# One more of the 22 gated pairs of the second feed-forward in seven products, its input sums beside one plain pair

## Chip, core and metric

The program runs on one core of a Trainium2 chip. The metric is the device time of one execution in microseconds (us), from the first instruction to the last and what lies around them. Lower is better. All inputs and outputs are fp32 and lie in the chip's memory.

The engines are named as the profile names them: PE multiplies matrices, DVE and ACT work on vectors (ACT also evaluates functions), POOL and SP here mostly start transfers. Every engine works through its own list of instructions in order.

## The reference

One step of a two-layer encoder over 1088 positions (1024 of a prompt, 64 of a sample) with 1024 channels. Layer 0 mixes by attention, layer 1 by a state-space model and a gated linear unit (GLU). Each layer then has a gated feed-forward with a causal convolution of width 3. The change is in the feed-forward of layer 1 and in what is prepared for it:

```python
def conv_ffn(h, prev, w_up, conv_w, conv_b, w_down):
    t = h.shape[1]
    up = h @ w_up
    full = jnp.concatenate([prev.astype(up.dtype), up], axis=1)
    c = conv_b
    for j in range(CONV_WIDTH):
        c = c + conv_w[j] * full[:, j:j + t]
    y = (jax.nn.gelu(c[..., :D_FF]) * c[..., D_FF:]) @ w_down
    return y, full[:, -(CONV_WIDTH - 1):]
...
    hp = rms_norm(xp, g_pre_ffn[i])
    fp, cpi = conv_ffn(hp, zeros, w_up[i], conv_w[i], conv_b[i], w_down[i])
    xp = xp + rms_norm(fp, g_post_ffn[i])
```

`w_up` is 1024 x 5632: 2816 gate columns and 2816 value columns, which are 22 + 22 tiles of 128. A gate tile f and its value tile 22 + f are a **pair**.

## The kernel before

Channels lie on the 128 partitions and positions along the free axis, in three blocks of 384, 384 and 320 positions. An fp32 factor is split into a high and a low half (`hh` and `hl` for the activations, the two halves of `whl` for a weight tile), and `mm3` (L221 to L225) makes a product of three matmuls: high weights by low activations (L223), high by high (L224), low weights by high activations (L225). The low half of a weight tile is made by DVE (L216) after ACT has made the high half, so the first two matmuls of a product can start without DVE and the third cannot. Weights come through `unit` (L166), which keeps two units loaded ahead through two buffers `raw` and six buffers `whl`.

**Plain pair** (`up`, `up_block`, L404 to L433): for each tile and block, 8 x 3 matmuls into one of six PSUM buffers `mm`; DVE then multiplies by the norm's factor `rb` (L414, L416) and thereby frees the buffer. `conv` (L418 to L425) follows with one pass on ACT and two on DVE (L423, L424), `gate` (L435) multiplies the two tiles (L440) and POOL stores the result to `gd`.

**Pair in seven products** (`seven`, L496): for the first two blocks (768 positions as two halves of 384, 1024 channels as two halves of 512) the 2 x 2 x 2 block product is made of seven products in place of eight, by sums of the inputs and sums of the weights. The third block stays plain. Sums of the inputs are made once, on DVE: `normed` (L462) multiplies the activations by the norm, `input_sums` (L470) makes four differences (L478) and the split of one of them, `into_place` (L483) splits the other operands into high and low (`split`, L458: ACT makes the high half at L459, DVE the low half at L460). Four of these overwrite `hh` and `hl` of the first two blocks, from which the plain pairs read until then. Sums of the weights are made during the GLU before it, by jobs of two halves per pair (`sums`, L1388): POOL loads `sj` (L1392), DVE makes four sums (L1396 to L1399), POOL stores them to `su` (L1400). One job starts with each of the 48 steps of the GLU (`beside`, L1405), and its sums stand two steps later; the GLU uses 34 such steps for 17 pairs.

The constant `PLAIN` (L29) says how many pairs are plain. In the loop over f in `ffn` (L537) with `PLAIN` = 5: pair 1 is plain; before pair 2 the first two blocks are normed; before pair 3 `input_sums` is issued; pair 4 is issued as two interleaved tiles (`up([f, KF + f])`, L543), then `into_place` and the norm of the third block; from pair 5 on every pair is `seven`, and the first of these still uses the third block as it was and is followed by the split of its normed form.

The order on each engine is made by the framework's scheduler from priorities and a timeline that it simulates while the program is built; the code fixes single edges (`order`, L112).

Of the kernel before, what the change touches and what calls it, by code (L numbers as in the profile page):

```python
# [25 lines left out]
LOW = 1500  # L26
SIDE = 32

PLAIN = 5  # L29

KCUT = (0, 12, 22)
GT = [[(4, "blkA")] * 3, [(4, "blkB"), (4, "blkB"), (2, "big")]]
# [11 lines left out]
class Core:  # L44
    def __init__(self, ctx, tc, a):
# [5 lines left out]
        for i in range(2):  # L51
            for m in range(KF):
                sums = [("w_sum", m, e) for e in range(2)] if i == 1 and m >= PLAIN else []
                self.wsrc += [("w_up", i, m)] + sums + [("w_up", i, m + KF)]
# [285 lines left out]
    def ffn(self, i, h, rb, after, side=None, beside=lambda: None, x=None, g=None):  # L340
# [12 lines left out]
        def sums_w(k):  # L353
            x = (jt[:, :2048] if i == 0 else self.yp.tile([P, 2048], F32, name="jw", tag="ypB", bufs=1)).rearrange("p (c h m) -> p c h m", c=2, h=2)
            Q.dma_start(x, a["w_down"][i, k::KH].rearrange("c p (h m) -> p c h m", h=2))
            yield
            a11, a12, a21, a22 = x[:, 0, 0], x[:, 1, 0], x[:, 0, 1], x[:, 1, 1]
            E.tensor_add(a22, a21, a22)
            E.tensor_sub(a21, a11, a21)
            E.tensor_sub(a11, a22, a11)  # L360
            E.tensor_sub(a12, a12, a11)
            Q.dma_start(sd[:, k], x)
# [16 lines left out]

        w0 = (PLAIN + 1) * i  # L380
        starts = {2 * (k + w0) + 1: sums_w(k) for k in range(KH)}
# [45 lines left out]
        def up(ms):  # L427

            wu = {m: up_start(m) for m in ms}
            for b in range(3):  # L430
                for w, u in wu.values():
                    up_block(w, u, b)
            return {m: u for m, (w, u) in wu.items()}  # L433
# [28 lines left out]
        def normed(bs):  # L462

            for b in bs:
                t0, n = BLK[b]
                for k in range(KD):
                    v = nc.vector.scalar_tensor_tensor(x[b][:, k], x[b][:, k], g[:, k:k + 1], rb[:, t0:t0 + n], op0=ALU.mult, op1=ALU.mult)
                    self.order(v, self.last_conv)

        def input_sums():  # L470

            V = nc.vector
            b11, b21, b12, b22 = (half(x[b], j) for b in range(2) for j in range(2))
            t1, t4 = (self.big([P, 4, 384], "t", F32) for _ in range(2))
            t2 = ts.tile([P, 4, 384], F32, name="t2", tag="t2")
            for o, u, v in ((t1, b12, b11), (b12, b22, b12), (t2, b22, t1), (t4, b21, t2)):
                for k in (slice(0, 2), slice(2, 4)):
                    self.order(V.tensor_sub(o[:, k], u[:, k], v[:, k]), self.last_conv)  # L478
            op["t1"] = [ts.tile([P, 4, 384], F32R, name=f"t1{j}") for j in range(2)]
            split(*op["t1"], t1)  # L480
            return t2, t4
# [14 lines left out]
        def seven(f, first):  # L496
            V = nc.vector
            ug, uv = u_tile(f), u_tile(KF + f)
            g0, g1, v0, v1 = (u[:, 2 + 384 * j:386 + 384 * j] for u in (ug, uv) for j in range(2))

            def product(w, j, o, sums=False):
                ps = self.mm_ps()[:, :384]
                for k in range(4):
                    c = (k // 2 * 4 + 2 * j + k % 2 if sums else 4 * j + k) * P
                    self.mm3(ps, w, slice(c, c + P), op[o][0][:, k], op[o][1][:, k], k == 0, k == 3)
                return ps
            w = self.unit(("w_up", i, f))
            if first:
                up_block(w, ug, 2)
            nc.scalar.activation(g1, product(w, 0, "b11"), AF.Copy)  # L510
            V.tensor_add(g0, g1, product(w, 1, "b21"))
            ws = self.unit(("w_sum", f, 0))
            V.tensor_add(g1, g1, product(ws, 0, "t2", True))
            p3 = product(ws, 1, "b22", True)
            if not first:
                up_block(w, ug, 2, True)
            ws = self.unit(("w_sum", f, 1))
            V.tensor_add(v1, g1, product(ws, 0, "t3", True))
            V.tensor_add(g1, g1, p3)
            p5 = product(ws, 1, "t1", True)  # L520
            V.tensor_add(g1, g1, p5)  # L521
            w = self.unit(("w_up", i, KF + f))
            V.tensor_add(v0, v1, product(w, 1, "t4"))
            V.tensor_add(v1, v1, p5)
            up_block(w, uv, 2, not first)
            return {f: ug, KF + f: uv}
# [10 lines left out]
        for f in range(1, KF):  # L537
            if i == 1 and f == 2:
                normed((0, 1))
            if i == 1 and f == 3:  # L540
                late = input_sums()
            if i == 1 and f == PLAIN - 1:
                us = up([f, KF + f])  # L543
                into_place(*late)
                normed((2,))
            if i == 1 and f >= PLAIN:
                us = seven(f, f == PLAIN)
                if f == PLAIN:
                    for j in range(2):
# [1060 lines left out]
```

## Time and profile before

| | us |
|---|---|
| median of 3 runs (2247.86 to 2254.37) | 2248.89 |
| the profiled execution | 2243.39 |
| its span, first to last instruction | 2241.6 |
| PE busy in the span | 2188.9 (98%) |
| DVE busy in the span | 1687.4 (75%) |
| ACT busy in the span | 1019.1 (45%) |

Times in the trace are counted from the first instruction. The GLU runs from about 1300 to 1492, the second feed-forward's plain pairs from 1492 to 1616, its pairs in seven products from 1616 to about 1988, and its down-projection after that. A row of the timeline has the start, the length, the engine, line and operation, what it writes and reads, and in brackets how long the engine was idle before it and what released it. Matmuls overlap one another by half their length, so the pace of PE is read from the distance of their starts, not from the length of one. On DVE, too, the next instruction starts up to 0.1 us before the end of the one ahead of it.

### The profile page before, as it was taken

How to read it: one execution, taken by the hardware profiler on the slowest of the kernel's cores; microseconds unless marked ns; L12 is line 12 of the kernel's file. 1: busy time of each engine (PE TensorE's matmuls, PEld its weight loads, DVE VectorE, ACT ScalarE, POOL GpSimd, SP SyncE). 2: the span in 40 equal slices, each digit the busy share in tenths (PEclk: the TensorE clock that was granted, in tenths of full speed). 3: DMA queues.
4: the chain of work that ended last, by engine and by line, in shares of the span. 5: the costliest groups of instructions: out<-in, count | busy, mean ns of one | idle time of the engine just before them, and what ended most of it. 6: DMA issues, size and time to landing. Idle time of an engine off the chain costs nothing.

```text
span 2241.6 us, 36077 instructions
## 1 busy us (share of the span) xinstructions
PE 2188.9 (98%) x13875; PEld 2114.0 (94%) x13875; DVE 1687.4 (75%) x2954; ACT 1019.1 (45%) x1839; POOL 414.7 (18%) x474
## 2 busy tenths in 40 slices
PE   9999999999999999999998899999999999999997
PEld 8987789999999999999996699999999999999997
DVE  8687648989877877666768865587997788786754
ACT  5256747422333333455534742263444444455543
POOL 5322004200042323100200034352011111110000
PEclk9999999999999999999999999999999999999999
DMA  5100015656345565887749998751266667678773
GB/s 197 38 22 29 20 62 158 246 184 211 111 136 183 181 192 184 253 298 232 229 147 340 272 295 297 261 167 65 96 217 223 236 237 276 209 269 310 224 243 99
DMA packets 208124, 428.48 MB, mean 191 GB/s; under 512 B 23312, under 2 KB 114224, under 8 KB 205008
## 3 DMA queue, kind: packets, MB, share of 16 engines
q1 hardware_dynamic: 175648, 326.56, 44.3%
q0 software_dynamic: 23984, 95.12, 11.9%
q10 hardware_dynamic: 8320, 4.49, 0.9%
q8 instruction: 109, 1.79, 0.3%
q14 instruction: 63, 0.52, 0.1%
HBM read 297.75 MB, written 128.37 MB: 190 GB/s over the span
## 4 chain that ended last, share of the span: by engine, by line
PE 47%; DMA 6%; DVE 5%; ACT 1%; issue 1%; SPq 1%; POOL 0%; DVEq 0%; ACTq 0%; POOLq 0%
PE mm L225 12%; PE mm L223 12%; PE mm L224 12%; DMA raw<-in_w_down 3%; PE pb L223 1%; PE pb L225 1%; PE pa L224 1%; PE pb L224 1%; PE pa L225 1%; PE pa L223 1%; DVE whl L216 1%; ACT whl L216 1%; DMA yd<-ys 1%; DMA pm<-prm 1%; DVE y L328 0%
## 5 line engine op out<-in xcount | busy, mean ns | idle before, releaser
L223 PE MATMUL mm<-hl,whl 128*128 128x384 f32 (+1 forms) x1960 | 643.4, 329 | 3.8 <-DVE hl L306 3.1
L225 PE MATMUL mm<-hh,whl 128*128 128x384 f32 (+1 forms) x1960 | 641.1, 328 | 2.2 <-DVE whl L216 2.2
L224 PE MATMUL mm<-hh,whl 128*128 128x384 f32 (+1 forms) x1960 | 642.3, 328 | 0.0
L223 PEld LDWEIGHTS mm<-hl,whl 128*128 128x128 f32 x1960 | 368.5, 188 | 6.0 <-DVE hl L306 4.5
L225 PEld LDWEIGHTS mm<-hh,whl 128*128 128x128 f32 x1960 | 368.5, 188 | 2.9 <-DVE whl L216 2.9
L224 PEld LDWEIGHTS mm<-hh,whl 128*128 128x128 f32 x1960 | 368.7, 188 | 0.0
L216 ACT ACTIVATE whl<-raw 128x1024 fp32r<-128x1024 f32 x202 | 212.9, 1058 | 333.4 <-PE mm L225 192.2
L216 DVE TENSOR_TENSOR whl<-raw,whl 128x1024 fp32r<-128x1024 f32 x202 | 254.9, 1264 | 111.2 <-ACT whl L216 110.7
L223 PE MATMUL mm<-gt,whl 128*128 128x384 f32 (+1 forms) x968 | 316.8, 327 | 2.6 <-ACT whl L216 1.7
L225 PE MATMUL mm<-gt,whl 128*128 128x384 f32 (+1 forms) x968 | 315.8, 327 | 0.7 <-DVE whl L216 0.7
L224 PE MATMUL mm<-gt,whl 128*128 128x384 f32 (+1 forms) x968 | 315.9, 327 | 0.0
L223 PEld LDWEIGHTS mm<-gt,whl 128*128 128x128 f32 x968 | 181.7, 188 | 3.2 <-ACT whl L216 1.9
L225 PEld LDWEIGHTS mm<-gt,whl 128*128 128x128 f32 x968 | 181.6, 188 | 1.2 <-DVE whl L216 1.2
L224 PEld LDWEIGHTS mm<-gt,whl 128*128 128x128 f32 x968 | 181.7, 188 | 0.0
L194 DVE TENSOR_TENSOR whl<-raw,whl 128x1024 fp32r<-128x1024 f32 x84 | 96.3, 1153 | 69.2 <-ACT whl L193 68.2
L193 ACT ACTIVATE whl<-raw 128x1024 fp32r<-128x1024 f32 x84 | 82.6, 987 | 115.0 <-DMA raw<-sd 50.2
L423 DVE SCALAR_TENSOR_TENSOR t<-u,ppt,t 128x1090 f32<-128x1090 f32 x88 | 123.6, 1407 | 7.9 <-ACT t L422 7.3
L422 ACT ACTIVATE t<-u,ppt 128x1090 f32<-128x1090 f32 x88 | 114.2, 1298 | 24.4 <-DVE u L521 9.2
L424 DVE SCALAR_TENSOR_TENSOR t<-u,ppt,t 128x1090 f32<-128x1090 f32 x88 | 123.3, 1403 | 0.4
L414 DVE TENSOR_TENSOR u<-rb,mm 128x384 f32<-128x384 f32 (+1 forms) x164 | 80.2, 502 | 20.4 <-PE mm L225 15.7
L566 DVE TENSOR_TENSOR gt<-gr,gt 128x768 fp32r<-128x768 f32 (+2 forms) x106 | 89.9, 879 | 7.1 <-ACT gt L565 6.8
L565 ACT ACTIVATE gt<-gr 128x768 fp32r<-128x768 f32 (+2 forms) x106 | 78.4, 773 | 35.6 <-DMA gr<-gd 24.6
(390 smaller groups left out, 4113.4 us busy)
## 6 DMA issues: line engine op xcount, KB each, us to landing
raw<-in_w_up SPq DMA_DIRECT2D x88, 512.0 KB, 4.2
raw<-in_w_down SPq DMA_DIRECT2D x74, 512.0 KB, 4.4
raw<-sd SPq DMA_DIRECT2D x40, 512.0 KB, 4.6
sj<-in_w_up POOLq DMA_DIRECT2D x68, 256.0 KB, 6.1
su<-sj POOLq DMA_DIRECT2D x34, 512.0 KB, 5.8
raw<-su SPq DMA_DIRECT2D x34, 512.0 KB, 4.7
pm<-prm SPq DMA_DIRECT2D x32, 522.0 KB, 8.6
gr<-td SPq DMA_DIRECT2D x40, 384.0 KB, 5.7
```

The lines of the kernel that those rows point to most:

```text
L193: nc.scalar.activation(w[:, 0], raw, AF.Copy)
L194: nc.vector.tensor_sub(w[:, 1], raw, w[:, 0].bitcast(F32))
L216: x = nc.scalar.activation(w[:, 0], raw, AF.Copy), nc.vector.tensor_sub(w[:, 1], raw, w[:, 0].bitcast(F32))
L223: nc.tensor.matmul(out, w[:, 0, sl], xl, start=start, stop=False)
L224: nc.tensor.matmul(out, w[:, 0, sl], xh, start=False, stop=False)
L225: self.last_mm = nc.tensor.matmul(out, w[:, 1, sl], xh, start=False, stop=stop)
L414: nc.vector.tensor_mul(u[:, t0 + 2:t0 + 2 + np_], rb[:, t0:t0 + np_], ps[:, :np_])
L422: nc.scalar.activation(t, u[:, 0:T + 2], AF.Identity, bias=cb(m), scale=cw(0, m))
L423: nc.vector.scalar_tensor_tensor(t, u[:, 1:T + 3], cw(1, m), t, op0=ALU.mult, op1=ALU.add)
L424: self.last_conv = nc.vector.scalar_tensor_tensor(t, u[:, 2:T + 4], cw(2, m), t, op0=ALU.mult, op1=ALU.add)
L565: nc.scalar.activation(x[:, 0, u], raw, AF.Copy)
L566: nc.vector.tensor_sub(x[:, 1, u], raw, x[:, 0, u].bitcast(F32))
```

## The change

`PLAIN` goes from 5 to 4:

```diff
-PLAIN = 5
+PLAIN = 4
```

Pair 4 becomes a pair in seven products. `input_sums`, the norm of the third block and `into_place` are now all issued with pair 3, which takes the interleaved form that pair 4 had. The GLU gets two more jobs of weight sums (36 in place of 34), the list of weight units gets two units of sums for pair 4, and the sums of the down-projection's weights (`sums_w`, started at L380 and L381) begin one pair earlier.

On PE, in the second feed-forward, this is the end of the last tile of pair 3 (weights `whl_15061` before, `whl_15077` after) and what follows it. Before:

```order
L225 MATMUL mm_15322<-hh_14515,whl_15061 128x320
L223 MATMUL mm_15373<-hl_14195,whl_15171 128x384
L224 MATMUL mm_15373<-hh_14194,whl_15171 128x384
L223 MATMUL mm_15399<-hl_14195,whl_15264 128x384
L224 MATMUL mm_15399<-hh_14194,whl_15264 128x384
L223 MATMUL mm_15425<-hl_14465,whl_15171 128x384
L224 MATMUL mm_15425<-hh_14464,whl_15171 128x384
L223 MATMUL mm_15451<-hl_14465,whl_15264 128x384
L224 MATMUL mm_15451<-hh_14464,whl_15264 128x384
L225 MATMUL mm_15373<-hh_14194,whl_15171 128x384
```

With the change:

```order
L225 MATMUL mm_15332<-hh_14531,whl_15077 128x320
L223 MATMUL mm_15406<-hl_14532,whl_15187 128x320
L224 MATMUL mm_15406<-hh_14531,whl_15187 128x320
L223 MATMUL mm_15433<-hl_14211,whl_15187 128x384
L224 MATMUL mm_15433<-hh_14210,whl_15187 128x384
L223 MATMUL mm_15447<-hl_14211,whl_15187 128x384
L224 MATMUL mm_15447<-hh_14210,whl_15187 128x384
L225 MATMUL mm_15406<-hh_14531,whl_15187 128x320
```

Before, pair 4 starts as two plain tiles with eight matmuls that need only high weights (`whl_15171` is tile 4). After, the third block of tile 4 (`mm_15406`) and its first two products start with six such matmuls (`whl_15187` is tile 4), and the seventh needs the low half.

On DVE, this is the stretch up to the split that makes that low half. The names: `y_12619`, `y_12658`, `y_12697` are the three blocks, `t_...`, `t2_...` the differences, `hl_`, `th_` and `t11_` low halves of operands. Before:

```order
L460 TENSOR_TENSOR t11_15166<-t_15154,t10_15165 128x1536
L478 TENSOR_TENSOR t_15155<-y_12619,t2_15156 128x768
L396 MEMSET u_15267 128x2
L414 TENSOR_TENSOR u_15267<-rb_14193,mm_15270 128x384
L216 TENSOR_TENSOR whl_15171<-raw_15169,whl_15171 128x1024
L216 TENSOR_TENSOR whl_15264<-raw_15262,whl_15264 128x1024
```

With the change:

```order
L460 TENSOR_TENSOR t11_15182<-t_15170,t10_15181 128x1536
L414 TENSOR_TENSOR u_15190<-rb_14209,mm_15253 128x384
L414 TENSOR_TENSOR u_15198<-rb_14209,mm_15279 128x384
L460 TENSOR_TENSOR hl_14481<-y_12658,hh_14480 128x1536
L414 TENSOR_TENSOR u_15190<-rb_14209,mm_15305 128x256
L416 TENSOR_TENSOR u_15190<-rb_14209,mm_15305 128x64
L414 TENSOR_TENSOR u_15198<-rb_14209,mm_15332 128x256
L416 TENSOR_TENSOR u_15198<-rb_14209,mm_15332 128x64
L478 TENSOR_TENSOR t_15171<-y_12619,t2_15172 128x768
L460 TENSOR_TENSOR hl_14481<-y_12658,hh_14480 128x1536
L478 TENSOR_TENSOR t_15171<-y_12619,t2_15172 128x768
L216 TENSOR_TENSOR whl_15187<-raw_15185,whl_15187 128x1024
```

Before, the split of tile 4's weights stood behind the split of `t11` and ahead of all splits of the other operands and of the norm of the third block. Now it stands behind all eight halves of differences (L478), behind four of the six splits that `into_place` makes (L460), and, above the rows shown, behind the eight multiplications that norm the third block (L467).

On DVE at the end of the GLU, this piece of the difference shows one of the two new jobs; `y<-pa,ppt,sg` is the last tile of the first block, and L256 and L260 finish the sum of squares of the norm for which PE waits in L266:

```order
 L1399 TENSOR_TENSOR sj<-sj 128x256
+L1396 TENSOR_TENSOR sj<-sj 128x256
+L1397 TENSOR_TENSOR sj<-sj 128x256
+L1398 TENSOR_TENSOR sj<-sj 128x256
+L1399 TENSOR_TENSOR sj<-sj 128x256
 L1438 SCALAR_TENSOR_TENSOR y<-pa,ppt,sg 128x384
 L256 TENSOR_TENSOR sqa<-sqa 128x768
 L260 TENSOR_TENSOR sqa<-sqa 128x384
```

Four sums are put ahead of the last tile's L1438. On POOL their two loads stand between stores of earlier jobs:

```order
 L1400 DMA su<-sj 128x1024
 L1392 DMA sj<-in_w_up 128x2x256 x2
-L1400 DMA su<-sj 128x1024 x3
+L1400 DMA su<-sj 128x1024
+L1392 DMA sj<-in_w_up 128x2x256 x2
+L1400 DMA su<-sj 128x1024 x2
+L1392 DMA sj<-in_w_up 128x2x256 x2
+L1400 DMA su<-sj 128x1024 x2
```

The loads of the first new job come directly behind the first of what were three stores in a row. On PE, L266 of that norm stands two matmuls later than before.

## The prediction, made before the changed kernel was run

> **What bounds the kernel now.** I read the page's busy shares first (PE 98%), then busy time by stage, then the timelines of DVE and PE around the pairs that change.
>
> ```profile
> 1545.00:2010.00 465.00, 465.00 (x2818) 465.00 (x2817) 388.97 (x515) 208.09 (x333) 50.35 (x86) 1.00 0.59 208
> 1568.37:1592.16 23.79, 23.79 (x146) 23.79 (x145) 22.14 (x32) 7.31 (x10) 2.09 (x4) 1.00 0.17 61
> 1592.16:1615.95 23.79, 23.79 (x147) 23.79 (x145) 22.34 (x29) 13.92 (x14) 1.07 (x2) 1.00 0.36 121
> 1659.37:1681.09 21.72, 21.72 (x135) 21.72 (x133) 19.32 (x24) 9.22 (x16) 2.48 (x5) 1.00 0.73 264
> ```
>
> The rows are windows (length, then busy time of PE, weight loads, DVE, ACT and POOL, then the granted clock, the share of the DMA engines and GB/s). PE never stops from 1545 to 2010: the stage is bound by PE, and what PE saves is saved. But the second and third rows, the plain pairs 3 and 4, show DVE busy for 22.14 and 22.34 of 23.79 us. It makes the sums of the inputs there and has 3.1 us left in two pairs. The change takes away one of the two.
>
> **What is saved.** The starts 1568.37 and 1592.16 are those of pairs 3 and 4, so a plain pair costs 23.79 us of PE. The fourth row is one pair in seven products, 21.72. One pair changes its kind: 23.79 - 21.72 = **2.07 us** saved, 0.09%. That is all that the change can bring, since no other matmul goes.
>
> **What DVE has to do before PE may go on.** Its timeline gives the prices, as distances between starts:
>
> ```profile
> 1574.06 1.35 DVE L423 SCALAR_TENSOR_TENSOR t<-u,ppt,t 128x1090 f32<-128x1090 f32 x1
> ...
> 1577.49 1.35 DVE L424 SCALAR_TENSOR_TENSOR t<-u,ppt,t 128x1090 f32<-128x1090 f32 x1
> 1578.75 1.82 DVE L478 TENSOR_TENSOR t<-y 128x768 f32<-128x768 f32 x2
> 1580.49 1.29 DVE L440 TENSOR_TENSOR t<-t 128x1090 f32<-128x1090 f32 x1
> 1581.69 0.95 DVE L478 TENSOR_TENSOR y<-y 128x768 f32<-128x768 f32 x1
> 1582.56 0.95 DVE L478 TENSOR_TENSOR t<-y,t 128x768 f32<-128x768 f32 x1
> 1583.43 0.42 DVE L414 TENSOR_TENSOR u<-rb,mm 128x256 f32<-128x256 f32 x1
> 1583.76 0.22 DVE L416 TENSOR_TENSOR u<-rb,mm 128x64 f32<-128x64 f32 x1
> 1583.89 0.95 DVE L478 TENSOR_TENSOR y<-y 128x768 f32<-128x768 f32 x1
> ...
> 1585.63 1.75 DVE L460 TENSOR_TENSOR t<-t,t 128x1536 fp32r<-128x1536 f32 x1
> 1587.30 0.95 DVE L478 TENSOR_TENSOR t<-y,t 128x768 f32<-128x768 f32 x1
> 1588.18 0.55 DVE L414 TENSOR_TENSOR u<-rb,mm 128x384 f32<-128x384 f32 x1
> ...
> 1588.65 2.35 DVE L216 TENSOR_TENSOR whl<-raw,whl 128x1024 fp32r<-128x1024 f32 x2
> 1590.92 0.95 DVE L478 TENSOR_TENSOR t<-y,t 128x768 f32<-128x768 f32 x1
> 1591.79 1.35 DVE L423 SCALAR_TENSOR_TENSOR t<-u,ppt,t 128x1090 f32<-128x1090 f32 x1
> 1593.05 0.88 DVE L414 TENSOR_TENSOR u<-rb,mm 128x384 f32<-128x384 f32 x2
> ...
> 1603.82 3.79 DVE L467 SCALAR_TENSOR_TENSOR y<-y,ppt,rb 128x320 f32<-128x320 f32 x8
> 1607.52 1.21 DVE L216 TENSOR_TENSOR whl<-raw,whl 128x1024 fp32r<-128x1024 f32 x1
> ```
>
> Prices: L423 and L424 1.26 each (1591.79 to 1593.05; 1577.49 to 1578.75), a half difference L478 0.87, a split L460 1.67, L440 1.20, L414 of 384 0.47, L414 with L416 of the third block 0.46, the norm L467 of the third block 3.70 for eight, two weight splits L216 2.27 and the first of them 1.21.
>
> Up to L423 at 1574.06 DVE's order is the same with the change, so I walk on from there on the time axis of before. Next in the new order is the first split of an operand, which waits for ACT, and ACT for PE:
>
> ```profile
> 1599.35 1.49 ACT L459 ACTIVATE hh<-y 128x1536 fp32r<-128x1536 f32 x1 [0.34 <-PE mm L225]
> 1592.16 0.34 PE L223 MATMUL mm<-hl,whl 128*128 128x384 f32 x1
> 1592.34 0.34 PE L224 MATMUL mm<-hh,whl 128*128 128x384 f32 x1
> ```
>
> ACT may overwrite the first four of the eight channel tiles of a block when the last plain tile has read them. A matmul of 384 takes 0.176 us from start to start (1592.16 to 1592.34), one of 320 takes 0.147. With pair 3 interleaved, its second tile reads the first block from 1568.37 + 24 x 0.176 = 1572.6, and the first twelve matmuls end the reading of those four at 1574.7. ACT's 1.49 us then end at about 1576.4, and DVE starts its split there, having waited 1 us.
>
> From 1576.4 to the split of tile 4's weights DVE has, by the new order: five L460 (8.35), eight L478 (6.96), L467 (3.70), one L424 (1.26), L440 (1.20), three L414 of 384 (1.41), two third blocks (0.92). The sum is 23.8 us, so L216 starts at 1600.2 and the low half of `whl` is there at **1601.4**. PE has finished pair 3 at 1592.16, as before (there the first row of 384 starts pair 4), and has six matmuls that need only the high half (2 x 0.147 + 4 x 0.176 = 1.0). It stands still from 1593.2 to 1601.4: **8.2 us**. In the profile of before the same split started at 1588.65 and was in time for 1592.16 by 2.3 us. The bounds of this term: 0, if DVE reached L216 by 1592; 10.6, if each of the 30 instructions cost 0.08 us more, the difference between its length and the distance of starts. Nothing excludes either end; the walk is nearest to the rows, so I take 8.2.
>
> What is late next: the third product needs the low half of its operand. DVE makes it after two L216, two L423 and one L460, at 1600.2 + 2.3 + 2.5 + 1.7 = 1606.7. PE gets there at 1601.4 + 22 x 0.147 + 20 x 0.176 = 1608.2, no wait. The sixth product needs the PSUM buffer of the third block's result, which DVE frees after another L460, two L424, two L216 and L414 with L416, at 1613.6; PE comes at 1612.7, so **0.9 us** would be lost, unless PE is slower by then. It may be, by what its clock does after standing still elsewhere in this trace:
>
> ```profile
> 1177.00:1181.30 4.30, 1.31 (x10) 1.03 (x9) 1.71 (x7) 2.13 (x7) 0.00 (x0) 1.00 1.02 420
> 1181.30:1184.70 3.40, 3.40 (x7) 1.55 (x6) 2.88 (x4) 1.99 (x5) 0.00 (x0) 0.50 0.54 219
> ```
>
> PE was busy for 1.31 of 4.30 us, and for the next 3.4 us the granted clock was 0.50. After 8.2 us without work I expect the same: 3.4 us at half clock lose **1.7 us**, bounds 0 and 3.4 (one such stretch more). This hides the 0.9, so the two together cost 1.7. The Trainium skill, "TensorE: Matmul & The Clock Gate", Part 1, states the rule behind it: the array's clock falls to half after an idle window of about 3.4 us and returns after a busy one. By that rule the restart is slow, without it the sum would be 0.8 us less; the trace agrees, with 0.50 for 3.4 us.
>
> **The end of the GLU.** Two more jobs of weight sums cost DVE eight instructions and POOL four loads and two stores, beside PE, except for the first job:
>
> ```profile
> 1438.23 1.42 POOL L1392 DMA_DIRECT2D sj<-in_w_up  x2 [1.28 <-DMA su<-sj]
> 1443.15 0.56 POOL L1400 DMA_DIRECT2D su<-sj  x1 [3.51 <-DVE sj L1399]
> DMA to landing us min/median/max: 3.4/6.1/9.8
> 1445.64 0.42 DVE L1398 TENSOR_TENSOR sj<-sj 128x256 f32<-128x256 f32 x1
> 1446.10 0.42 DVE L1399 TENSOR_TENSOR sj<-sj 128x256 f32<-128x256 f32 x1
> 1446.45 0.61 DVE L1438 SCALAR_TENSOR_TENSOR y<-pa,ppt,sg 128x384 f32<-128x384 f32 x1
> 1447.97 0.96 DVE L256 TENSOR_TENSOR sqa<-sqa 128x768 f32<-128x768 f32 x1 [0.91 <-ACT sqa L254]
> 1448.96 0.56 DVE L260 TENSOR_TENSOR sqa<-sqa 128x384 f32<-128x384 f32 x1
> 1450.45 0.72 PE L266 MATMUL pr<-ones,sqa 128*128 128x1 f32 x6
> ```
>
> The new loads follow the store of 1443.15 on POOL, so the second is issued at 1443.15 + 0.56 + 0.7 = 1444.4. With the least landing time of these loads, 3.4 us, it is there at 1447.8, with the median at 1450.5. Few loads are under way then, so I take 1447.8. Four sums of 0.46 follow (1445.64 to 1446.10), and only then L1438, at 1449.65 instead of 1446.45. L260 ended 3.07 us after L1438's start (1446.45 to 1448.96 + 0.56), now at 1452.7. PE reaches L266 at 1450.45 + 2 x 0.176 = 1450.8, so it waits **1.9 us**, bounds 1.9 and 4.6. What waits behind L266 is PE's whole list. The second job's sums stand ahead of L276, 9 us before PE needs its result: no cost.
>
> **Sum:** -2.07 + 8.2 + 1.7 + 1.9 = **+9.7 us**. Against the profiled execution, 2243.39, this is 2253.1, or 0.43%. That execution lies 5.5 us below the median of the runs shown; I put the same 9.7 on the median, 2248.89 + 9.7 = **2258.6 us**. A run of this kernel can be told from another by about 0.3%, 6.75 us.
>
> **Rivals.**
>
> 1. *No wait at tile 4: not slower.* The whole gain would be the 2.07 us and the loss at most the GLU's 1.9, so -2.1 to 0 us, 2246.8 to 2249. For it: in the profile of before PE has no wait there at all, with DVE nearly as full. Against it: DVE has to start L216 of tile 4 by 1592, 8 us earlier than the walk, and its list is fixed, so it can't take the split first. It decides at 1592. Chance 0.10.
> 2. *Half the wait.* If ACT's first split and the L414 come without waits and the clock stays up, 8.2 may be 3 to 6, and the sum +1 to +6.7: 2250 to 2255.6. Chance 0.18.
> 3. *DVE stays behind.* In a seven-product pair DVE is busy for 19.32 of 21.72 us. A debt carried into pairs 5 and 6 is paid back at 2.4 us a pair, and each later weight split can stop PE again; with the GLU's loads at the median, the sum is +13 to +20: 2262 to 2269. Against it: while PE stands still DVE catches up 8 us. Chance 0.14.
>
> The forecast, +6.8 to +13, keeps 0.58. The range from 2250.5 to 2266 leaves out rival 1, the lower edge of 2 and the end of 3, together 0.2. Slower by over 0.3%: the forecast and rival 3, less what lies near the bound, 0.70. Within 0.3%: 0.27. Faster by over 0.3% has no mechanism here: 0.03.
>
> **What would show it.** In the changed profile PE's waits should have one of about 8 us at L225 for `whl` L216 behind pair 3, the granted clock should be 0.50 for 3.4 us behind it, DVE should be without idle time from 1576 to that point, and L266 at the end of the first GLU block should wait 2 us for DVE. A plain pair fewer and 21.7 us for pair 4 without the wait confirm the gain. The forecast is wrong if the split of tile 4's weights starts before PE asks for it, or if PE's later pairs wait too.

## The result and the profile after

The change makes the kernel slower. In the first comparison the median is 2262.97 us (2254.86 to 2271.62, 11 runs) against 2244.20 before (2239.82 to 2254.37, 11 runs): a ratio of 1.0076, 95% interval 1.0062 to 1.0089, or +13.9 to +20.0 us. A second comparison, later, gave 2250.44 against 2241.68, a ratio of 1.0040 (1.0027 to 1.0054), +6.1 to +12.1 us. The forecast was +9.7 us, put on a median of three runs (2248.89), so 2258.6, with a range of 2250.5 to 2266.

The profiled execution of the change took 2266.74 us, its span is 2265.0. Busy time by stage first (length, then busy time of PE, weight loads, DVE, ACT and POOL, then the granted clock, the share of the DMA engines and GB/s). The rows are the GLU, the up part of the second feed-forward, and its down-projection, before:

```profile
1299.15:1492.71 193.56, 193.56 (x1180) 193.51 (x1180) 118.55 (x250) 66.03 (x99) 84.34 (x112) 1.00 0.77 261
1492.71:1985.07 492.36, 491.82 (x2994) 490.94 (x2993) 411.78 (x561) 220.98 (x361) 70.27 (x96) 1.00 0.56 196
1985.07:2227.40 242.33, 241.36 (x1472) 240.79 (x1470) 154.60 (x194) 122.69 (x163) 12.59 (x12) 1.00 0.72 239
```

and after:

```profile
1305.79:1506.50 200.71, 196.44 (x1180) 196.07 (x1180) 122.72 (x260) 66.80 (x100) 88.33 (x118) 0.98 0.77 262
1506.50:2005.85 499.35, 491.31 (x2982) 489.80 (x2980) 411.72 (x559) 223.07 (x367) 70.05 (x96) 0.99 0.55 193
2005.85:2249.80 243.95, 242.25 (x1472) 240.60 (x1470) 155.74 (x195) 122.79 (x163) 12.13 (x12) 1.00 0.73 242
```

The up part has grown from 492.36 to 499.35 us although PE has fewer matmuls (2982 rows for 2994). The GLU takes 200.71 us in place of 193.56. In both stages PE now stands still: the timeline of PE after the change has one wait of over 2 us in each, and a short one just ahead of the second:

```profile
1461.81 1.44 PE L266 MATMUL pr<-ones,sqa 128*128 128x1 f32 x6 [4.27 <-DVE sqa L260]
1607.34 0.44 PE L223 MATMUL mm<-hl,whl 128*128 128x384 f32 x1 [0.49 <-DVE u L414]
1614.93 0.64 PE L225 MATMUL mm<-hh,whl 128*128 128x320 f32 x1 [6.98 <-DVE whl L216]
```

The third row is the wait that the prediction is built on: 6.98 us, behind pair 3, for the low half of tile 4's weights. DVE's timeline ahead of it:

```profile
1589.86 1.76 DVE L460 TENSOR_TENSOR hl<-y,hh 128x1536 fp32r<-128x1536 f32 x1 [0.99 <-ACT hh L459]
...
1594.54 3.78 DVE L467 SCALAR_TENSOR_TENSOR y<-y,ppt,rb 128x320 f32<-128x320 f32 x8
...
1612.79 0.95 DVE L478 TENSOR_TENSOR t<-y,t 128x768 f32<-128x768 f32 x1
1613.66 2.35 DVE L216 TENSOR_TENSOR whl<-raw,whl 128x1024 fp32r<-128x1024 f32 x2
```

From the first split of an operand to L216 it is 1613.66 - 1589.86 = 23.80 us, the 23.8 of the walk, and the split waited 0.99 us for ACT (forecast 1). The windows of pairs 3, 4 and 5 after the change:

```profile
1581.83:1605.93 24.10, 23.97 (x147) 23.71 (x145) 23.07 (x34) 11.03 (x12) 2.09 (x4) 1.00 0.12 47
1605.93:1637.07 31.14, 23.66 (x132) 23.02 (x133) 28.99 (x36) 14.21 (x18) 1.07 (x2) 0.89 0.34 119
1637.07:1658.73 21.66, 21.66 (x134) 21.66 (x133) 20.37 (x26) 11.51 (x17) 1.82 (x3) 1.00 0.60 197
```

Pair 4 takes 31.14 us; the forecast was 21.72 + 8.2 + 1.7 = 31.6. Pair 5 is back at 21.66, and PE has no wait in it or in any pair behind it: DVE catches up while PE stands still.

### The profile page after: what moved, and what is told of

The parts are those of the page before. It is cut to its first block, busy times and chain, and to the rows that moved or that the text cites. A ratio compares the mean times of both kernels' runs of the same rounds, so it can differ in the third digit from the quotient of the medians.

```text
span 2265.0 us, 36098 instructions
## 1 busy us (share of the span) xinstructions
PE 2194.9 (97%) x13863; PEld 2117.4 (93%) x13863; DVE 1691.9 (75%) x2963; ACT 1022.4 (45%) x1846; POOL 417.0 (18%) x480
## 5 line engine op out<-in xcount | busy, mean ns | idle before, releaser
L225 PE MATMUL mm<-hh,whl 128*128 128x384 f32 (+1 forms) x1944 | 636.7, 328 | 9.2 <-DVE whl L216 9.2
L225 PEld LDWEIGHTS mm<-hh,whl 128*128 128x128 f32 x1944 | 366.0, 188 | 10.2 <-DVE whl L216 10.2
L216 ACT ACTIVATE whl<-raw 128x1024 fp32r<-128x1024 f32 x204 | 214.8, 1058 | 346.5 <-PE mm L225 152.8
L216 DVE TENSOR_TENSOR whl<-raw,whl 128x1024 fp32r<-128x1024 f32 x204 | 256.8, 1265 | 120.9 <-ACT whl L216 120.5
L225 PE MATMUL mm<-gt,whl 128*128 128x384 f32 (+1 forms) x968 | 316.4, 327 | 0.7 <-DVE whl L216 0.7
L225 PEld LDWEIGHTS mm<-gt,whl 128*128 128x128 f32 x968 | 182.1, 188 | 1.2 <-DVE whl L216 1.2
L423 DVE SCALAR_TENSOR_TENSOR t<-u,ppt,t 128x1090 f32<-128x1090 f32 x88 | 123.6, 1405 | 8.2 <-ACT t L422 7.7
L331 POOL TENSOR_TENSOR y<-y,xl 128x768 f32<-128x768 f32 (+1 forms) x16 | 30.0, 1872 | 334.5 <-DVE y L328 269.7
```

Of the source, the lines that this page charges most:

```text
L216: x = nc.scalar.activation(w[:, 0], raw, AF.Copy), nc.vector.tensor_sub(w[:, 1], raw, w[:, 0].bitcast(F32))
L225: self.last_mm = nc.tensor.matmul(out, w[:, 1, sl], xh, start=False, stop=stop)
L331: x = by[q].tensor_add(yq, yq, xs[q])
L423: nc.vector.scalar_tensor_tensor(t, u[:, 1:T + 3], cw(1, m), t, op0=ALU.mult, op1=ALU.add)
```

## Experiments

All were timed beside the kernel before on the same chip. "Up part" is the stage of 492.36 us, "GLU" the one of 193.56 us, both from the profiled execution. Each expectation sets a theory against one or more rivals.

**1. The kernel before again, as a control.**

> The kernel before, unchanged, as a control. The ratio should be 1.000 with an interval of some 0.002 to each side. Its trace tells what varies from one execution to another without any change: if the first stages (up to the GLU) or the down-projection differ from the first trace of before by 2 to 6 us, then such differences in the other traces are not the change's. If the variation is under 1 us in each stage, the 5 us that the kernel with only the GLU's jobs lost in its down-projection need a cause in the change.

Measured: ratio 1.0001 (0.9992 to 1.0010). The GLU took 193.56 us again, the up part 492.61, the down-projection (to its last matmul) 241.5 where the first trace has 242.0. From the GLU to that point nothing thus varied by over 0.5 us. Up to the GLU's first matmul it took 1296.6 us, where the first trace has 1299.2. In the eleven other traces of kernels run here, whose instructions are the same up to the GLU, this start lies between 1290.9 and 1299.3; in the first trace of the change it is 1305.8. No edit stands ahead of the GLU, and the same kernel's second trace (experiment 12) has the earliest start of all, 1290.9. So the 6.6 us by which the first trace is behind when it reaches the GLU are not put down to the change; what made them is not shown.

**2. The GLU's jobs alone.**

```diff
-jobs = iter([sums(f, e) for f in range(PLAIN, KF) for e in range(2)])
+jobs = iter([sums(f, e) for f in range(PLAIN - 1, KF) for e in range(2)])
```

with `PLAIN` = 5.

> The kernel before with the two extra jobs of weight sums in the GLU; pair 4 stays plain and their result is not used. Theory (the loss is made in two places, and about half of it at the end of the GLU): PE waits 4 to 5 us for DVE L260 at L266, the granted clock is 0.50 for some 6 us from that wait on, and the kernel is 6 to 7.5 us slower than before, ratio about 1.003. Rival A (the landing time of 5.3 us in the changed kernel's trace was one execution's): the wait is 2 us, the clock stays 1.00, and the time is 0 to 2 us above before, ratio below 1.001. Rival B (the feed-forward alone makes the loss): no wait at L266 and no difference.

Measured: ratio 1.0040 (1.0021 to 1.0060). In its trace L266 waits only 1.17 us and the clock stays up; the GLU is 1.3 us longer, the up part as before:

```profile
1451.99 0.83 PE L266 MATMUL pr<-ones,sqa 128*128 128x1 f32 x6 [1.17 <-DVE sqa L260]
1299.06:1493.93 194.87, 193.70 (x1179) 193.33 (x1180) 123.03 (x260) 66.61 (x100) 88.29 (x118) 1.00 0.79 270
1493.93:1985.89 491.96, 491.53 (x2993) 490.99 (x2992) 405.80 (x554) 218.16 (x357) 70.19 (x96) 1.00 0.55 192
1985.89:2233.50 247.61, 243.96 (x1472) 242.15 (x1470) 158.82 (x199) 125.20 (x165) 12.55 (x12) 0.99 0.73 240
```

The time follows the theory, the wait in the GLU's trace rival A, and the rest of that execution's loss lies in the down-projection (247.61 for 242.33), where nothing was edited. The GLU's wait is 1.17 us here and 4.27 in the first trace of the change.

**3. The same jobs, the last two started three steps later.** The change with

```diff
-jobs = iter([sums(f, e) for f in range(PLAIN, KF) for e in range(2)])
+jobs = iter([sums(f, e) for f in range(PLAIN, KF) for e in range(2)][:34] + [iter(())] * 3 + [sums(KF - 1, e) for e in range(2)])
```

> The change with the last two jobs of weight sums started three steps later in the GLU, so that none of their sums stands ahead of the norm of the first block (L256, L260) in DVE's list. Theory: no wait at L266 of the first block beyond that of before (0 to 0.5 us), the clock stays 1.00 there, the GLU is as long as before within 1 us, the feed-forward's wait of 7 us stays; the whole is 7 to 10 us slower than before, ratio 1.003 to 1.0045, against 1.0076 of the change. Rival (loads and stores of the sums hinder the GLU wherever they stand): a wait of 1 us or more at L266 or elsewhere in the GLU, ratio 1.005 or more.

Measured: ratio 1.0045 (1.0029 to 1.0060). L266 no longer waits, the GLU is that of before, and the feed-forward's wait is the same to 0.01 us:

```profile
1450.07 0.72 PE L266 MATMUL pr<-ones,sqa 128*128 128x1 f32 x6
1601.10 0.64 PE L225 MATMUL mm<-hh,whl 128*128 128x320 f32 x1 [6.98 <-DVE whl L216]
1298.82:1492.31 193.49, 193.49 (x1180) 193.44 (x1181) 122.40 (x259) 66.45 (x100) 87.34 (x118) 1.00 0.80 271
1492.31:1992.04 499.73, 491.54 (x2982) 489.77 (x2981) 410.98 (x560) 222.75 (x367) 70.27 (x96) 0.99 0.55 192
```

As expected: the GLU's part hangs on the place of the last jobs and not on their number. The down-projection, to its last matmul, took 244.8 us.

**4. The late jobs in the kernel before.** The same edit with `PLAIN` = 5 and the two more jobs of experiment 2 (`range(PLAIN - 1, KF)`).

> The kernel before with the two extra jobs of weight sums in the GLU, started three steps later, their result not used: the same instructions as in the kernel with the GLU's jobs alone, which was 1.0040 of before, but for their place. Theory (that loss was the wait at L266 with its half clock): no wait at L266, GLU as long as before, ratio 0.999 to 1.001. Rival (the extra loads and stores shift something for all that follows, such as the waits of the down-projection): GLU as before, down-projection 2 to 5 us longer, ratio 1.001 to 1.003.

Measured: ratio 1.0013 (1.0000 to 1.0026), GLU 193.48, up part 492.46, down-projection 242.0. The wait is gone, as the theory has it; the time is a little above the theory's 1.001, and the longer down-projection that the rival asks for is not in the trace. By these two experiments some 0.27% of the 0.40% of experiment 2 is the place of the two jobs, and from their intervals this may be anything from nearly 0 to 0.5%; the rest is at the edge of what can be measured.

**5. The feed-forward's part, with the jobs early.** The change with two jobs started in one step at steps 8 and 14 of the GLU:

```diff
-            loaded.append(next(jobs, iter(())))
-            next(loaded[-1], None)
-            if len(loaded) > 2:
+            for _ in range(2 if next(calls) in (8, 14) else 1):
+                loaded.append(next(jobs, iter(())))
+                next(loaded[-1], None)
+            while len(loaded) > 2:
```

> The change with the two extra jobs started earlier in the GLU, at its steps 8 and 14, so that DVE's list at the end of the GLU is that of before. Theory: L266 waits for nothing, and the wait of 7 us for the split L216 of tile 4's weights with the 3 us at half clock behind it stays; the kernel is 6 to 8 us slower than before, ratio about 1.003, and 7 us faster than the change. Rival A (the GLU's part was an accident of one execution): same time as the change, ratio 1.006 to 1.009. Rival B (the feed-forward's wait grew only because the GLU ended late): less than 3 us slower than before, ratio below 1.0015.

Measured: ratio 1.0049 (1.0030 to 1.0067). The feed-forward is as the theory has it (L225 waits 6.98 us, up part 501.13), but L266 waits 2.71 us, although DVE's order around it is that of before. The second load ahead of the last sums was issued 143.4 us after the GLU's first matmul, in place of 139.8 before, and landed at 149.3 in place of 145.6. The theory fell for the GLU: taking the new sums out from ahead of L1438 is not enough when the last loads come later.

**6. The input sums one pair earlier.**

```diff
-            if i == 1 and f == 2:
+            if i == 1 and f == PLAIN - 3:
                 normed((0, 1))
-            if i == 1 and f == 3:
+            if i == 1 and f == PLAIN - 2:
                 late = input_sums()
```

> The change with the norm of the first two blocks issued before pair 1 and the input sums before pair 2, so that they have pairs 2 and 3 beside them, as they had pairs 3 and 4 before. The GLU is that of the change. Theory (DVE has too much to do beside one plain pair): no wait for L216 behind pair 3, the clock stays 1.00 there, the feed-forward's up part is 2 us shorter than before, the GLU's loss of 7 us stays: 4 to 6 us slower than before, ratio about 1.002. Rival (the sums cost the same wherever they stand, since one plain pair fewer is left in all): a wait of 5 us or more appears in pairs 1 to 4, ratio 1.005 or more.

Measured: ratio 1.0062 (1.0047 to 1.0076), up part 498.20. The theory fell, and the rival holds, with four waits in place of its one. The wait of 7 us is gone, and four others stand in pairs 2 and 3, together 5.9 us, three of them for PSUM buffers that DVE frees in L414:

```profile
1559.79 0.45 PE L223 MATMUL mm<-hl,whl 128*128 128x384 f32 x1 [1.83 <-DVE u L414]
1574.19 0.44 PE L223 MATMUL mm<-hl,whl 128*128 128x384 f32 x1 [1.24 <-DVE u L414]
1576.32 0.44 PE L223 MATMUL mm<-hl,whl 128*128 128x320 f32 x1 [1.52 <-DVE u L414]
1578.32 0.69 PE L225 MATMUL mm<-hh,whl 128*128 128x384 f32 x1 [1.29 <-DVE whl L216]
1540.00:1583.00 43.00, 37.11 (x208) 35.80 (x207) 40.05 (x56) 16.58 (x23) 2.23 (x4) 0.93 0.12 41
```

DVE is busy for 40.05 of 43 us there. With the sums beside two pairs the up part is still 5.8 us longer than before, against 7.0 to 8.9 with the change: while there are only four plain pairs, most of the loss stays.

**7. Experiments 5 and 6 together.**

> The change with both edits: the two jobs earlier in the GLU and the input sums one pair earlier. Theory (the two waits are the whole loss): no wait at L266 and none for L216 behind pair 3; 0 to 3 us faster than before, ratio 0.9985 to 1.000, which the measurement may not tell from no change. Rival (something else in the change costs as well, such as the earlier start of the down-projection's weight sums): 2 us or more slower than before, ratio 1.001 or more.

Measured: ratio 1.0059 (1.0043 to 1.0076); up part 498.54 and GLU 198.15, which is what 6 and 5 showed one by one (498.20 and 198.07). The theory fell: L266 waits 2.80 us, and pairs 2 and 3 have three waits of 1.4 to 1.9 us.

**8. Tile 4's split first.** The splits of `into_place` and the norm of the third block are tied behind the split of `whl` for tile 4 (`split_ops` lists the weight splits, and tile 4's is the last but one when they are issued). The split of its first unit of sums, which the expectation names too, is not tied; in the trace it stands ahead of the splits of `into_place` and behind the norm. Cut:

```diff
+        self.split_ops = getattr(self, "split_ops", []) + [x]
...
-        def split(hi, lo, src):
+        def split(hi, lo, src, first=()):
...
+            for u, v in zip(x, first): self.order(u, v)
...
-                    self.order(v, self.last_conv)
+                    self.order(v, self.split_ops[-2][1] if b == 2 else self.last_conv)
...
-                split(hi, lo, src)
+                split(hi, lo, src, self.split_ops[-2])
```

> The change with the splits of tile 4's weights and of its first unit of sums fixed ahead of the third block's norm and of the operands' splits, on ACT and DVE. Theory A (what stands behind is late next): DVE reaches the split of tile 4's weights 6 us before PE asks for it, no wait at L225 behind pair 3; PE then waits 4 to 5 us before the third product for the low half of its operand (L223 for DVE L460), and the feed-forward's up part is 2 to 5 us longer than before, in place of 7. Theory B (only the order was bad): no wait of over 1 us anywhere, the up part is 1 to 2 us shorter than before. Theory C (DVE's work is the bound, the order moves nothing): waits of 7 us in all, up part 7 to 9 us longer.

Measured: ratio 1.0051 (1.0034 to 1.0069), up part 498.43. In PE's and DVE's timelines the split is ready early and PE waits at the third product:

```profile
1587.28 1.22 DVE L216 TENSOR_TENSOR whl<-raw,whl 128x1024 fp32r<-128x1024 f32 x1
1607.06 0.69 PE L223 MATMUL mm<-th,whl 128*128 128x384 f32 x1 [6.19 <-DVE th L459]
```

(L459 is in this kernel the line of the low half that is L460 elsewhere.) Theory A had the place right and the size too low (4 to 5), and with 6.19 in place of 6.98 us theory C is as near; theory B fell. The order is worth 0.8 us of the wait, and 0.9 to 2.8 us of the up part (499.35 to 501.24 with the change); most of the loss stays with the length of DVE's list.

**9. Less work for DVE: 3.7 us.** The change without `normed((2,))`. This kernel leaves out the norm of the third block and serves as a probe only.

> The change without the norm of the third block (eight L467 of DVE, 3.7 us), so that the third block of the pairs in seven products is computed from activations that are not normed. Theory (PE waits for the length of DVE's list, one to one): the wait at L225 for the split of tile 4's weights is 7.0 - 3.7 = 3.3 us, the half clock behind it is shorter or gone, and the feed-forward's up part is 2 to 4 us longer than before, in place of 7 to 9. Rival (the split waits for something else, such as its load or ACT): the wait stays within 1 us of 7.

Measured: ratio 1.0027 (1.0011 to 1.0042), up part 492.80:

```profile
1593.03 0.41 PE L225 MATMUL mm<-hh,whl 128*128 128x320 f32 x1 [1.43 <-DVE whl L216]
1607.36 0.45 PE L223 MATMUL mm<-t,whl 128*128 128x384 f32 x1 [0.72 <-ACT u L510]
```

DVE's timeline of this kernel, from the first split of an operand to L216:

```profile
1574.65 1.76 DVE L460 TENSOR_TENSOR hl<-y,hh 128x1536 fp32r<-128x1536 f32 x1 [0.99 <-ACT hh L459]
...
1591.75 1.23 DVE L216 TENSOR_TENSOR whl<-raw,whl 128x1024 fp32r<-128x1024 f32 x1
```

That is 17.10 us in place of 23.80, 6.7 less: the norm's 3.7, and 3.0 of a half difference (0.87), a split (1.67) and a third block (0.46) that the order, made anew, now has behind L216. PE's wait falls from 6.98 to 1.43, by 5.55 and not by 6.7, since PE comes 1.1 us earlier too: it asks for the low half 17.0 us after that first split begins (1593.03 - 1.43 - 1574.65), in place of 18.1. The rival fell, and the theory's 3.3 us were too many because it took the order for fixed. The clock stays up, and the up part is 6.6 us shorter than in the first trace of the change.

**10. Less work for DVE: 11.1 us.** Experiment 3 without any of the norms ahead of the input sums (`for b in ()` in `normed`); like experiment 9, it leaves out work that the result needs.

> The change with the late jobs of the GLU and without the norms that stand ahead of the input sums (24 instructions L467 of DVE, 11.1 us), so that the pairs in seven products are computed from activations that are not normed. The split of tile 4's weights then stands in DVE's list with 11.1 us less ahead of it than in the change, where PE waited 7.0 us for it. Theory (the gain of the change is there, and DVE's list alone hides it): no wait of over 0.5 us behind pair 3, the clock 1.00, the up part 490.3 us, 2.1 less than before's 492.4; the GLU 193.5 as before; the whole 0 to 3 us faster than before, ratio 0.9985 to 1.000. Rival (other waits take its place, as in the kernel that lacked only the third block's norm, where 2.5 us were left): up part 492 to 493, ratio 1.000 to 1.002. The down-projection is left open by both: 241.5 to 242.0 in three executions with the plain pairs of before, 240.5 to 247.3 in the others.

Measured: ratio 0.9998 (0.9989 to 1.0007), GLU 193.48:

```profile
1488.22:1979.55 491.33, 489.89 (x2981) 488.74 (x2980) 403.11 (x538) 224.31 (x368) 70.33 (x96) 1.00 0.57 198
1602.69 0.44 PE L223 MATMUL mm<-t,whl 128*128 128x384 f32 x1 [0.76 <-ACT u L510]
```

The up part is 1.03 us shorter than before's 492.36, between the theory (490.3) and the rival (492 to 493); the time is the theory's. Of the 2.07 of the plain pair, 0.76 go to one wait in pair 4 for a PSUM buffer, here freed by ACT; 0.3 us are not placed. With 11.1 us less in DVE's list, half of the saving shows.

**11. The norms on ACT and POOL.** Experiment 3, the norms for the first two blocks issued at pair 1, and

```diff
-v = nc.vector.scalar_tensor_tensor(x[b][:, k], x[b][:, k], g[:, k:k + 1], rb[:, t0:t0 + n], op0=ALU.mult, op1=ALU.mult)
-self.order(v, self.last_conv)
+self.order(nc.scalar.activation(x[b][:, k], x[b][:, k], AF.Copy, scale=g[:, k:k + 1]), self.last_conv)
+nc.gpsimd.tensor_mul(x[b][:, k], x[b][:, k], rb[:, t0:t0 + n])
```

> The change with the late jobs of the GLU, and with the norms of the three blocks for the input sums taken off DVE: ACT multiplies by the gain, POOL by the norm's factor, the first two blocks issued one pair earlier. DVE loses 24 instructions of 11.1 us in the plain pairs. Theory (DVE's list is the only bound there): no wait for L216 behind pair 3 and none of over 1 us in the up part, which is 1 to 2 us shorter than before; the GLU as long as before; the whole within 2.5 us of before, ratio 0.998 to 1.001. Rival A (POOL's multiplications slow DVE down, or the stores of gated pairs, now behind them on POOL, hold buffers): waits of 2 us or more in pairs 1 to 4, ratio 1.001 to 1.004. Rival B (the down-projection loses in the changed kernels too): the up part as in the theory, but the down-projection 2 to 5 us longer than before.

Measured: ratio 1.0064 (1.0048 to 1.0080), up part 506.41, 14 us longer than before. Rival A, and more than its ratio of 1.001 to 1.004: PE has four waits of 2.2 to 2.8 us in pairs 3 and 4. The timelines of POOL and DVE:

```profile
1548.77 11.79 POOL L468 TENSOR_TENSOR y<-y,rb 128x384 f32<-128x384 f32 x11
```

```profile
1548.70 10.99 DVE L423 SCALAR_TENSOR_TENSOR t<-u,ppt,t 128x1090 f32<-128x1090 f32 x1 [2.38 <-ACT t L422]
```

One L423 of DVE, 1.35 us elsewhere, takes 10.99 us while POOL works through eleven multiplications (L468), the first ten of them 1.0 us each. It begins 0.07 us ahead of them and ends during the last, which takes 2.06 us. In a later stretch, from 1574.95 to 1585.23, both engines are slowed instead: six of POOL's multiplications take 1.4 to 2.4 us, and DVE's L478 up to 1.6 in place of 0.95. The Trainium skill, "SBUF — State Buffer", "SBUF: two separate sides", says that DVE and POOL share a pair of ports, held by one of them for a whole instruction while the other is blocked. The trace agrees that one blocks the other, and shows DVE blocked for ten POOL instructions in a row, though its row begins first. The rival's other half, that the stores behind the multiplications on POOL hold buffers, was not tried apart. Here the work taken off DVE was no relief on POOL.

**12. The change again.**

> The change, unaltered, beside the other kernels. In five traces with this order of the GLU so far its length above before was 1.1, 1.3, 2.9, 7.2 and 7.4 us, and the up part of the second feed-forward with this order was 7.0 to 8.8 us longer. Theory: the up part is again 7 to 9 us longer, with the same gap of 7.3 us at L225, the GLU anywhere from 1 to 7.5 us longer, and the ratio is 1.006 to 1.009. If the up part's gap differs by over 0.5 us, it depends on loads and not on DVE's list alone.

Measured: ratio 1.0040 (1.0027 to 1.0054). L225 waits 6.97 us, the up part is 501.24, the GLU 195.32 with 1.50 us at L266. The up part is 1.9 us longer than the first trace's 499.35; 1.3 of that is the clock, and 0.5 a wait in L266 at its start. The first row is from the first trace of the change, the second from this one, each the half clock behind the wait:

```profile
1614.90:1617.90 3.00, 2.97 (x11) 2.97 (x12) 3.00 (x3) 0.87 (x1) 0.00 (x0) 0.51 0.58 188
```

```profile
1595.33:1600.89 5.56, 5.56 (x21) 5.56 (x22) 5.56 (x5) 1.99 (x3) 0.00 (x0) 0.50 0.57 189
```

After the same wait the clock is at half for 3.0 us once and for 5.6 us the other time.

## Why the prediction was right, and where its size was off

| part | forecast, us | first trace of the change | second trace |
|---|---|---|---|
| up to the GLU | 0 | +6.6 | -5.7 |
| GLU | +1.9 | +7.2 | +1.8 |
| up part | +7.8 | +7.0 | +8.6 |
| down-projection and end | 0 | +2.6 | +6.0 |

(The first trace is set against the first trace of before, the second against the control's.)

**The saving.** Forecast 2.07 us. The traces bear it out in the main: pair 5 is at 21.66 us, and with DVE relieved (experiment 10) the up part is 1.03 us shorter with 0.76 us more of waiting in it.

**The wait at tile 4.** Forecast 8.2 us at L225 for L216. It stands there in all four executions of this feed-forward (experiments 3, 5 and 12 and the first trace), with 6.98, 6.98, 6.97 and 6.98 us. DVE's walk was right to the tenth (23.80 us, begun 8.03 us after the start of pair 3, forecast 8.0). Experiments 8, 9 and 10 show that it is the cause: when DVE's order changes PE still waits 6.19 us, at the third product; when 3.7 and 11.1 us of its norms are left out, the wait falls to 1.43 us and to none. What the walk lacked is that PE itself comes 1.2 us later: pair 3 takes 24.10 us in place of 23.79, and PE loses 0.5 us for a PSUM buffer that DVE frees in L414, at the fifth of the six matmuls that the walk let run free. (The rest is that the wait is counted from the end of the last matmul, and the walk went by starts.)

**The clock behind it.** Forecast 3.4 us at half speed, 1.7 lost. Measured 3.0 and 5.6 us, so 1.5 and 2.8 lost, both inside the bounds of 0 and 3.4. The rule that the prediction weighed from the Trainium skill, "TensorE: Matmul & The Clock Gate", Part 1, has the clock return after at least one busy window of about 3.4 us; the first trace is near one such window with 3.0, the second needed longer after the same gap. The PSUM wait of 0.9 us that the half clock was to hide does not show in the first trace; where the clock stayed up (experiments 9 and 10), a wait of 0.7 to 0.8 us shows at the sixth product, as the prediction placed it, but for a buffer that ACT frees and not DVE. Together the up part was forecast at -2.07 + 8.2 + 1.7 = +7.8 and measured +7.0 to +8.9.

**The end of the GLU is the term that was mis-sized.** Forecast 1.9 us, bounds 1.9 to 4.6, with the least landing time of 3.4 us, since "few loads are under way then". The new sums do stand ahead of L1438, and experiments 3 and 4 show that the wait goes when these sums are put behind it. But POOL's and DVE's timelines of the first trace have:

```profile
1450.38 0.56 POOL L1400 DMA_DIRECT2D su<-sj  x1 [4.58 <-DVE sj L1399]
1450.93 1.41 POOL L1392 DMA_DIRECT2D sj<-in_w_up  x2
```

```profile
1456.97 0.42 DVE L1396 TENSOR_TENSOR sj<-sj 128x256 f32<-128x256 f32 x1 [3.20 <-DMA sj<-in_w_up]
1458.69 0.61 DVE L1438 SCALAR_TENSOR_TENSOR y<-pa,ppt,sg 128x384 f32<-128x384 f32 x1
1461.20 0.56 DVE L260 TENSOR_TENSOR sqa<-sqa 128x384 f32<-128x384 f32 x1
```

The second load was issued at about 1451.6 and its sums began at 1456.97, 5.3 us later. The issue stands behind a store that had waited 4.58 us for the sums of an earlier job. Load, sums, store and next load are one chain, so a late landing makes a later load late. And the forecast gave no clock to this wait: after 4.27 us without a matmul PE worked at half speed,

```profile
1463.10:1467.60 4.50, 4.50 (x15) 4.50 (x16) 3.91 (x15) 3.97 (x8) 0.56 (x1) 0.50 0.30 120
```

which loses 2.25 us more. Over the six executions with this place of the jobs the wait was 0.9, 1.2, 1.2, 1.5, 4.3 and 4.4 us, and the GLU 1.1 to 7.4 us longer, 3.6 in the mean. In all six this load took 4.9 to 5.8 us to land, and in none the 3.4 of the forecast. In the two with the long waits it was issued 145.4 and 145.8 us after the GLU's first matmul, where the forecast has 145.2; in the other four it was issued at 142.5 to 143.3, which made up for the slower landing. So a forecast of 1.9 us among waits of 0.9 to 4.4 is in part luck: the landing was taken too short and, in four of six, the issue too late.

**The down-projection** was forecast at 0. It took 242.0, 241.5 and 242.0 us to its last matmul in the two traces of before and in experiment 4, 243.6 to 247.3 in the four executions with the feed-forward of the change, but also 247.3 in experiment 2, whose feed-forward is that of before, and 240.5 in experiment 8. The earlier start of the sums of its weights, which the change brings, does not do it alone: experiments 9 and 10 have that too and took 242.2 and 241.4 us. Short waits for PSUM buffers come and go there, and in experiments 2, 3 and 12 the clock is at half for 3.4 us behind one of them. The two traces of before repeat to 0.5 us there, so the edits may have a part in it that no run singles out. What sets these waits was not tried and stays open; it may be 2 to 5 of the 17 us at the middle of the first interval.

**The rivals.** Rival 1, no wait at tile 4, fell: 7 us are there in four traces. Rival 2, half the wait, fell too, as L225's wait does not vary. So did rival 3, DVE staying behind: from pair 5 on PE does not wait. The first comparison's +17 lies in rival 3's band all the same, without its mechanism: in the one trace taken there, what came on top of the forecast is the GLU's wait with its clock, the down-projection, and the 6.6 us ahead of the GLU.

**What was luck in the total.** The forecast was put on 2248.89, and over eleven runs the kernel before is at 2244.20. So 2262.97 is only 4.4 us above the forecast time, while the difference of the two medians, 18.8 us, is nearly twice the 9.7. The second comparison's 8.8 us is near 9.7, but in its trace -5.7 us ahead of the GLU and +6.0 from the down-projection on cancel, neither of which was forecast. All eleven runs of the change in the first comparison (from 2254.86) lie above all six of the second (up to 2252.43). Why is not shown: their two traces differ most ahead of the GLU, by 14.9 us, where nothing was edited. What the traces do bear out is the up part, +7.8 forecast and +7.0 to +8.9 measured.

No version that computes the whole beats the kernel before; the nearest, experiment 4 at 1.0013, makes the sums for the eighteenth pair without using them.

## What to carry to other kernels

A second engine that is nearly full in a stage (here DVE, 22.1 of 23.8 us in pair 3) decides what the first may save there: before taking work from the bound engine, add up the list that must be done in the shorter time. Here changes of the order moved the wait and took little off it. Work put in front of a short chain for which the bound engine stands still (here four sums ahead of a norm) can cost the landing of its loads, and then the clock behind the wait. Price a wait as its length plus half of the stretch at half clock.

## What the runs showed of the hardware that was not expected

- A DVE instruction with two operands in SBUF was held for 10.99 us in place of 1.35 while POOL ran multiplications of about 1 us back to back (experiment 11). DVE got no turn between the first ten of them; in another stretch of the same trace both were slowed, POOL's multiplications to 1.4 to 2.4 us.
- The stretch at half clock after the same gap in PE's work (6.98 and 6.97 us) was 3.0 us in one execution and 5.6 us in another. The Trainium skill, "TensorE: Matmul & The Clock Gate", Part 1, says that the window that is watched runs freely and that the number of slow matmuls varies from run to run; the two traces agree, with 11 and 21 matmuls in these stretches.
- A wait fixed by DVE's list repeated to 0.01 us in four executions on at least two chips; a wait fixed by a chain of loads varied between 0.9 and 4.4 us over six executions with the same order.
